# Prompt attention with undivided probabilities: the reciprocals of the sums go through memory, and the results of a pair of heads are multiplied by them

## The chip, the cores and the metric

The kernel runs on one core of one Trainium2 chip. The metric is the device time of one execution in microseconds (us). A core has a matrix engine (PE, with a separate sequence of weight loads, PEld), a vector engine (DVE), an engine for activation functions and copies (ACT), a general one (POOL), and one that mostly issues transfers (SP). A transfer (DMA) is issued by the instruction stream of one of these engines; the rows call the issuing side ACTq, SPq and so on. Memory is DRAM; work happens in the core's own SBUF, and the PE writes into PSUM banks.

## The reference

One step of a layer with two feed-forward halves, a mixer, and norms around each, for a prompt of 1024 positions and a group of samples. Its mixer has a forgetting attention with 8 heads of 64, and a gated linear attention. The part that matters here is the forgetting attention of the prompt:

```python
def fox_prompt(q, k, v, logf):                   # B=1, T=1024, H=8, D=64
    c = jnp.swapaxes(jnp.cumsum(logf, axis=1), 1, 2)
    ...
        s = (jnp.einsum('bqhd,bkhd->bhqk', qb, k) * scale
             + cb[..., :, None] - c[..., None, :])
        mask = (start + jnp.arange(Q_BLOCK))[:, None] >= k_pos[None, :]
        p = jax.nn.softmax(jnp.where(mask, s, -jnp.inf), axis=-1)
        return jnp.einsum('bhqk,bkhd->bqhd', p, v)
```

All of it is float32. The softmax divides each row of exponentials by its sum before the product with `v`.

## The kernel before, in words

**The main stream.** The kernel walks through feed-forward half 1, projection, mixer output and feed-forward half 2. Nearly all of its PE time is matrix products with weights (`mm`, L230). A weight tile of 128x1024 arrives raw from memory (`wr`, 2 buffers), is split by ACT into a rounded part (`wh`, a cast, L213, 3 buffers) and by DVE into the rest (`wl`, L213, 3 buffers); the PE then multiplies with both parts.

**Background pieces.** Prompt attention does not have a stage of its own. It is written as Python generators that `yield` after each small piece. As the main stream advances, it calls `tick(us)` with its own estimate of the time of what it just wrote; that adds to a due count, and for each whole unit of the count one piece of the background is written. `together` takes one piece from each of its generators in turn. Prompt attention for the query chunks 0 and 1 (`fox((0, 1), ...)`, L2083) is written beside the projection, with the linear attention joining later; chunks 2 and 3 (`fox((2, 3), ...)`, L1774) are written beside the second feed-forward half, in turn with the linear attention `gla`. After everything has been written, a scheduler chooses the order of the instructions of each engine; each engine then works strictly in its own order.

**One head of attention.** A chunk has 256 queries, two blocks of 128. For a head h and a chunk c:

- `fox_load` has SP load keys and queries (`ka`, `kb`, `qa`, `qb`), and values (`v`) for every second head.
- `fox_scores`, once per block i: the PE writes the scores `s` (128 queries x n keys, L1429 to L1432; n is 128 to 1024). The DVE takes the maximum (L1434), ACT the exponential into `p` with the sum of each row beside it (L1435), the DVE the reciprocal of that sum (L1436), and ACT multiplies all of `p` by that reciprocal, one per partition (L1437). There are 2 buffers of `p` (`fp`).
- `fox_turn`: the PE transposes up to four 128x128 pieces of `p` into the one PSUM bank `tp` (L1447), and ACT copies them to `pT` (L1449). There are 96 such copies.
- `fox_out`: the PE multiplies `v` with `pT` into `po` (L1463): 64 rows (the head's dimensions) x 256 queries; except in chunk 0, the even and the odd blocks of keys are summed in the two halves of the partitions. ACT copies one half to SBUF (`pl`, L1468), and DVE adds the other (L1469); in chunk 0 ACT copies alone (L1465). An even head goes to partitions 0 to 63 and an odd one to 64 to 127 of one tile, so a pair of heads makes one tile of 128x256.

For chunks 0 and 1 that tile is a part of the next stage's input, `y` (the `put` of L2083's caller). For chunks 2 and 3 it is a tile `mo` with 2 buffers, and after an odd head `done` has SP store it to `mixd` in memory (L1768); `mixd` is loaded as the next stage's input when the attention is over.

There are 4 chunks x 8 heads x 2 blocks = 64 blocks, 32 heads and 16 pairs.

Of the kernel before, what the change touches and what calls it, by code (L numbers as in the profile page):

```python
# [8 lines left out]
F32 = mybir.dt.float32  # L9
# [3 lines left out]
AF = mybir.ActivationFunctionType  # L13
ALU = mybir.AluOpType
# [4 lines left out]
P = 128  # L19
# [41 lines left out]
def together(*gens):  # L61

    live = list(gens)
    while live:
        for g in list(live):
            if next(g, live) is live:
                live.remove(g)
            else:
                yield
# [819 lines left out]
class StepA(Step):  # L889
    def setup_a(self):  # L890
        cp, nc = self.const, self.nc
        dr = self.dram
        self.qs = dr.tile([2, 4, P, T], F32, name="qs")
        self.ks = dr.tile([2, 4, P, T], F32, name="ks")
        self.vs = dr.tile([4, P, KB, P], F32, name="vs")
        self.vss = dr.tile([4, TS, P], F32, name="vss")
        self.augs = dr.tile([8, 2, TP], F32, name="augs")
        self.cns = dr.tile([2, 8, TS], F32, name="cns")
        self.afs = dr.tile([2, 8, NB * NPG, P], F32, name="afs")
        self.gqs = dr.tile([2, P, T], F32, name="gqs")  # L900
        self.gks = dr.tile([2, P, T], F32, name="gks")
        self.gbs = dr.tile([2, P, T], F32, name="gbs")
        self.ggs = dr.tile([4, P, T], F32, name="ggs")
        self.gvs = dr.tile([9, P, 512], F32, name="gvs")
        self.zero = cp.tile([P, 1], F32, name="zero")
        nc.vector.memset(self.zero, 0.0)
        self.gS = cp.tile([P, 2, P], F32, name="gS")
        self.cend = cp.tile([8, 4], F32, name="cend")

# [430 lines left out]
QC = [(0, 256), (256, 256), (512, 256), (768, 256)]  # L1340
# [15 lines left out]
class StepB(StepA):  # L1356
# [57 lines left out]
            nc.sync.dma_start(self.v[:, :nk // P, :], self.vs[h // 2, :, :nk // P, :])  # L1414
        return ka, kb, qa, qb, self.v

    def fox_scores(self, c, i, ld, B, w):

        nc = self.nc
        ka, kb, qa, qb, _ = ld  # L1420
        g = QC[c][0] // P + i
        n = (g + 1) * P
        qs = slice(i * P, i * P + P)
        sp = self.ps.tile([P, w], F32, name=self.uid("s2"), tag="S", bufs=1024 // w)
        p = B.tile([P, w], F32, name=self.uid("p"), tag="p", bufs=self.fp)
        for o in range(0, n, 512):
            m = min(512, n - o)
            end = o + m == n
            nc.tensor.matmul(sp[:, o:o + m], qa[:, qs], ka[:, o:o + m], start=True, stop=False)  # L1429
            nc.tensor.matmul(sp[:, o:o + m], qb[:, qs], kb[:, o:o + m], start=False, stop=not end)  # L1430
            if end:
                nc.tensor.matmul(sp[:, g * P:n], self.identr, self.cmask, start=False, stop=True)  # L1432
        mx = B.tile([P, 4], F32, name=self.uid("fm"), tag="fm", bufs=4)
        nc.vector.tensor_reduce(out=mx[:, 0:1], in_=sp[:, :n], op=ALU.max, axis=AX.X, negate=True)  # L1434
        nc.scalar.activation(out=p[:, :n], in_=sp[:, :n], func=AF.Exp, bias=mx[:, 0:1], accum_out=mx[:, 1:2])  # L1435
        nc.vector.reciprocal(mx[:, 2:3], mx[:, 1:2])  # L1436
        nc.scalar.activation(out=p[:, :n], in_=p[:, :n], func=AF.Copy, scale=mx[:, 2:3])  # L1437
        return p

    def fox_turn(self, c, i, k0, p, pT):  # L1440
# [10 lines left out]
    def fox_out(self, c, h, v, pT, B, put):  # L1451

        nc = self.nc
        q0 = QC[c][0]
        e = h % 2
        r, x = slice(64 * e, 64 * e + 64), slice(64 - 64 * e, 128 - 64 * e)
        po = self.aux("po")
        last = q0 // P + 1
        one = last == 1
        for k in range(last + 1):  # L1460
            s = slice(0, 256) if k < last else slice(P, 256)
            out = po[r if one or k % 2 == 0 else x, s]
            nc.tensor.matmul(out, v[:, k, r], pT[:, k, s], start=(k == 0 or (k == 1 and not one)), stop=(k == last or (k == last - 1 and not one)))  # L1463
        if one:
            nc.scalar.copy(put(r, h // 2, q0), po[r, :256])  # L1465
            return
        t = B.tile([P, 256], F32, name=self.uid("pl"), tag="pl", bufs=1)
        nc.scalar.copy(t[r], po[x, :256])  # L1468
        nc.vector.tensor_tensor(out=put(r, h // 2, q0), in0=po[r, :256], in1=t[r], op=ALU.add)  # L1469

    def fox(self, cs, B, put, w, done=None):

        heads = [(c, h) for c in cs for h in range(8)]
        todo = [(k, i) for k in range(len(heads)) for i in range(2)]
        order = list(todo)
        loads, probs, turned = {}, {}, set()

        def issue():
            if not todo:
                return False  # L1480
            k, i = todo[0]
            j = order.index((k, i))
            if j - self.fp >= 0 and order[j - self.fp] not in turned:
                return False
            del todo[0]
            probs[k, i] = self.fox_scores(*heads[k][:1], i, loads[k], B, w)
            if i == 1 and k + 1 < len(heads):
                loads[k + 1] = self.fox_load(*heads[k + 1], B, w)
            return True

        loads[0] = self.fox_load(*heads[0], B, w)
        yield
        yield
        while issue():
            yield
        for k, (c, h) in enumerate(heads):
            pT = B.tile([P, w // P, 256], F32, name=self.uid("pT"), tag="pT", bufs=2)
            for i in range(2):
                for k0 in range(0, QC[c][0] // P + i + 1, 4):
                    self.fox_turn(c, i, k0, probs[k, i], pT)  # L1500
                    yield
                turned.add((k, i))
                while issue():
                    yield
            self.fox_out(c, h, loads[k][4], pT, B, put)
            if done is not None and h % 2:
                done(h // 2, QC[c][0])
            yield

    def gla_prep(self, ti, B):  # L1510

# [230 lines left out]
    def second(self, p4):  # L1742

        nc = self.nc
        self.ps, closep = self.pool("psX", space=PSUM)
        X, close = self.pool("X", side="right")
        self.rate = RATES
        yield from self.sample(X, self.ps)
        nc.sync.dma_start(self.mixd[:, :4, TP - HALF:], self.mixs)
        close()  # L1750
        p4.close_pages()
        closep()
        self.ps, closep = self.pool("psB1", space=PSUM)
        B, close = self.pool("B1", side="right")
        self.rate = RATE1
        self.naux, self.fp = 2, 2
        self.setup_b(B, TP)
        self.states(B)
        yield
        mo = {}  # L1760

        def put(r, a, q0):
            if r.start == 0:
                mo[a] = B.tile([P, 256], F32, name=self.uid("mo"), tag="mo", bufs=2)
            return mo[a][r]

        def done(a, q0):
            nc.sync.dma_start(self.mixd[:, a, q0 - HALF:q0 - HALF + 256], mo[a])  # L1768

        def gput(ti, t):  # L1770
            o = ti * P - HALF
            nc.sync.dma_start(self.mixd[:, 4:, o:o + t.shape[-1]], t)

        yield from together(self.fox((2, 3), B, put, TP, done), self.gla((4, 5, 8, 6, 7), B, gput))  # L1774
        close()
        closep()
        self.ps, _ = self.pool("ps5", keep=True, space=PSUM)
        self.banks = dict(col=("col", 1), col2=("col", 1), rows=("rows", 1))
        self.ncw, self.ssb, self.xb = NCW, 3, XB
        R, _ = self.pool("R", keep=True, side="right")  # L1780
        self.ub = [R.tile([P, KB, H1N], F32R, name=f"ub2{i}") for i in range(2)]
        p4.y = R.tile([P, KB, H1N], F32, name="y1")
        p4.R = R
        for c0, n in CH[2:]:
            s = slice(c0 - HALF, c0 - HALF + n)
            nc.sync.dma_start(p4.y[:, :, s], self.mixd[:, :, s])
        for _ in range(4):
            yield
        for c0, n in CH[2:]:
            s = slice(c0 - HALF, c0 - HALF + n)  # L1790
            for a in range(0, KB, 2):
                self.split(self.ub[0][:, a:a + 2, s], self.ub[1][:, a:a + 2, s], p4.y[:, a:a + 2, s])
                yield
# [467 lines left out]
```

## Time and profile before

| what | value |
|---|---|
| median of 3 runs | 2278.36 us |
| lowest and highest | 2270.86 and 2279.23 us |
| the profiled execution, its own time | 2268.31 us |
| its span (first to last instruction) | 2266.5 us |
| granted clock of the PE | 0.999 |

The profile is of one execution. Its busy times are per engine; issuing instructions are not counted as busy. A row of the waits view reads "who waited <- for what: us in total, times, longest". A row of the timeline or of the chain reads "start us, length us, what". A row of a line's view reads "engine, instruction, count: shortest/median/longest ns, first to last start". A matmul's end is modelled, so a PE that seems busy may be waiting for short moments; waits of the weight loads (PEld) show more of that.

### The profile page before, as it was taken

The numbers are of one execution on the slowest core, as the hardware profiler recorded it, in microseconds if no ns is written. First come the engines' busy times: TensorE is split into PE (matmuls) and PEld (weight loads), VectorE is DVE, ScalarE is ACT, GpSimd is POOL, SyncE is SP. The second block draws the span as 40 slices with busy tenths as digits, with TensorE's granted clock in tenths as the row PEclk, the third lists the DMA queues.
The fourth block names the chain that finished last, engine by engine and source line by source line (L and its number), as shares of the span: only waits on it lengthen the run. The fifth ranks groups of instructions, "written<-read, shape, count | busy, mean of one in ns | idle before, by whom it ended". The sixth has DMA issues, their size and how long they took to land.

```text
span 2266.5 us, 40596 instructions
## 1 busy us (share of the span) xinstructions
PE 2221.6 (98%) x15056; PEld 1982.9 (87%) x15056; DVE 1538.3 (68%) x2678; ACT 1031.2 (45%) x1787; POOL 625.8 (28%) x570
## 2 busy tenths in 40 slices
PE   9999999999999999999999999999999999999998
PEld 8898888999999877889898677777777989999998
DVE  7878886876777875476455333357775588678866
ACT  6544445433344465655345322236565546333433
POOL 2433332442223322011322312311110135234412
PEclk9999999999999999999999999999999999999999
DMA  5332223322233576564556899855554553224324
GB/s 185 123 103 98 98 99 130 98 82 88 93 113 124 166 256 194 182 191 128 188 181 203 300 346 333 316 159 146 166 151 137 194 174 114 97 89 140 103 83 137
DMA packets 201991, 357.26 MB, mean 158 GB/s; under 512 B 27265, under 2 KB 100546, under 8 KB 201410
## 3 DMA queue, kind: packets, MB, share of 16 engines
q1 hardware_dynamic: 185890, 316.36, 43.1%
q0 software_dynamic: 6544, 21.50, 2.6%
q10 hardware_dynamic: 9360, 16.81, 2.1%
q8 instruction: 120, 1.97, 0.4%
q14 instruction: 77, 0.63, 0.1%
HBM read 308.93 MB, written 45.65 MB: 156 GB/s over the span
## 4 chain that ended last, share of the span: by engine, by line
PE 48%; DVE 7%; issue 5%; ACT 3%; DMA 2%; POOL 1%; ACTq 0%; SPq 0%; DVEq 0%; POOLq 0%
PE mm L230 32%; PE mm L698 3%; DVE wl L213 3%; PE mx L698 2%; PE po L1463 1%; PE sp L1201 1%; PE po L1239 1%; PE tp L1447 1%; ACT wh L213 1%; DMA wr<-in_wd 1%; PE pa L1596 1%; PE s L1429 1%; PE s L1430 1%; PE pS L1639 1%; DMA wr<-in_wout 0%
## 5 line engine op out<-in xcount | busy, mean ns | idle before, releaser
L213 DVE TENSOR_TENSOR wl<-wr,wh 128x1024 fp32r<-128x1024 f32 (+1 forms) x251 | 290.2, 1158 | 181.3 <-ACT wh L213 179.7
L230 PE MATMUL mm<-ua,wh 128*128 128x512 f32 (+2 forms) x1328 | 412.1, 393 | 1.0 <-ACT ua L213 0.6
L213 ACT CAST wh<-wr 128x1024 fp32r<-128x1024 f32 (+1 forms) x251 | 245.2, 979 | 315.0 <-PE mm L230 165.2
L230 PE MATMUL mm<-ub,wh 128*128 128x256 f32 (+3 forms) x1760 | 371.6, 306 | 1.8 <-ACT st L968 0.8
L230 PE MATMUL mm<-hl,wh 128*128 128x256 f32 (+2 forms) x1006 | 330.8, 330 | 0.7 <-DVE hl L213 0.6
L230 PE MATMUL mm<-hh,wh 128*128 128x256 f32 (+2 forms) x958 | 320.7, 336 | 9.6 <-DVE y L646 5.7
L230 PE MATMUL mm<-hh,wl 128*128 128x256 f32 (+2 forms) x958 | 315.6, 330 | 2.2 <-DVE wl L213 2.2
L230 PEld LDWEIGHTS mm<-ub,wh 128*128 128x128 f32 (+1 forms) x1760 | 281.8, 189 | 11.7 <-issue 5.3
L230 PEld LDWEIGHTS mm<-ua,wh 128*128 128x128 f32 (+1 forms) x1328 | 237.3, 188 | 56.8 <-issue 13.1
L230 PE MATMUL mm<-ub,wl 128*128 128x256 f32 (+2 forms) x864 | 258.5, 299 | 1.0 <-DVE wl L213 1.0
L698 PE MATMUL mm<-ub,wh 128*128 128x288 f32 (+1 forms) x1328 | 258.3, 290 | 0.0
L230 PE MATMUL mm<-ua,wl 128*128 128x512 f32 (+1 forms) x656 | 252.1, 385 | 0.0
L698 PEld LDWEIGHTS mm<-ub,wh 128*128 128x128 f32 x1328 | 210.9, 189 | 0.0
L646 DVE TENSOR_TENSOR y<-y,mm 128x256 f32<-128x256 f32 (+2 forms) x275 | 137.0, 524 | 108.4 <-PE mm L230 108.1
L230 PEld LDWEIGHTS mm<-hh,wh 128*128 128x128 f32 x958 | 181.0, 189 | 31.1 <-issue 7.4
L230 PEld LDWEIGHTS mm<-hl,wh 128*128 128x128 f32 x1006 | 190.5, 190 | 15.0 <-DVE hl L213 1.8
L230 PEld LDWEIGHTS mm<-hh,wl 128*128 128x128 f32 x958 | 181.5, 189 | 16.8 <-DVE wl L213 3.7
L698 PE MATMUL mm<-ub,wl 128*128 128x288 f32 (+1 forms) x664 | 192.8, 290 | 0.0
L698 PE MATMUL mm<-ua,wh 128*128 128x288 f32 (+1 forms) x912 | 177.9, 290 | 0.8 <-ACT wh L213 0.8
L230 PEld LDWEIGHTS mm<-ub,wl 128*128 128x128 f32 x864 | 163.1, 189 | 2.8 <-DVE wl L213 1.4
L230 PEld LDWEIGHTS mm<-ua,wl 128*128 128x128 f32 x656 | 123.4, 188 | 26.6 <-issue 2.4
L698 PEld LDWEIGHTS mm<-ua,wh 128*128 128x128 f32 x912 | 144.6, 189 | 1.3 <-ACT wh L213 1.0
(336 smaller groups left out, 4189.1 us busy)
## 6 DMA issues: line engine op xcount, KB each, us to landing
wr<-in_wgu SPq DMA_DIRECT2D x72, 512.0 KB
wr<-in_wd SPq DMA_DIRECT2D x68, 512.0 KB
pr<-in_ck SPq DMA_DIRECT2D x112, 256.0 KB
wz<-in_wgu SPq DMA_DIRECT2D x100, 256.0 KB
wr<-in_win SPq DMA_DIRECT2D x50, 512.0 KB
pr<-in_cv ACTq DMA_DIRECT2D x64, 256.0 KB
wx<-in_wgu SPq DMA_DIRECT2D x50, 256.0 KB
wr<-in_wout SPq DMA_DIRECT2D x24, 512.0 KB
```

Of the source, the lines that this page charges most:

```text
L213: for ins in (self.nc.scalar.copy(hi, src), self.nc.vector.tensor_tensor(out=lo, in0=src, in1=hi.bitcast(F32), op=ALU.subtract)):
L230: ins = self.nc.tensor.matmul(*a, **kw)
L646: self.note(nc.vector.tensor_tensor(out=yk, in0=yk, in1=pds[d2, c0, e], op=ALU.add))
L698: nc.tensor.matmul(ps, a, x, start=(k == 0 and j == 0), stop=(k == KB // 2 - 1 and j == len(ops) - 1))
L1201: nc.tensor.matmul(sp[32 * a:32 * a + 32, 256 * hf:256 * hf + 256], qz[p % 2][:, a, s, :], raw[:, :, a * P:(a + 1) * P], start=False, stop ...
L1239: nc.tensor.matmul(po[r], pT[:, t, r], raw[:, :, a * P:(a + 1) * P], start=(t == 0), stop=False)
L1429: nc.tensor.matmul(sp[:, o:o + m], qa[:, qs], ka[:, o:o + m], start=True, stop=False)
L1430: nc.tensor.matmul(sp[:, o:o + m], qb[:, qs], kb[:, o:o + m], start=False, stop=not end)
L1447: nc.tensor.transpose(tp[:, k * P:(k + 1) * P], p[:, (k0 + k) * P:(k0 + k + 1) * P], self.ident)
L1463: nc.tensor.matmul(out, v[:, k, r], pT[:, k, s], start=(k == 0 or (k == 1 and not one)), stop=(k == last or (k == last - 1 and not one)))
L1596: nc.tensor.matmul(pa[:n, l - l0, :, a, :n // 2], E[:, l, a, :n], self.qd[:, l, a, :, :n // 2], start=True, stop=True)
L1639: nc.tensor.matmul(pS[:, a, :], km[:n, a, :], v[:n, a * 256:(a + 1) * 256], start=True, stop=True)
```

## The change

The exponentials are no longer divided. Instead:

- After the reciprocal, ACT issues a transfer of the 128 reciprocals of the block (one float32 per partition) to `rec`, a new tensor of 4 x 8 x 256 floats in memory, where the 256 of a head lie in a row.
- Ahead of `fox_out`, ACT issues a transfer that reads the head's row of `rec` into 64 partitions of a tile of 128x256, each partition getting the same row. An even head fills the lower half, an odd head the upper. The tile takes the name `pl` and the one buffer that the copy of `fox_out` had.
- `fox_out` now copies the one half straight to the place of the result, and adds the other half there.
- `whole` multiplies the tile of a pair by the tile of reciprocals: one DVE instruction of 128x256 per pair. In chunks 2 and 3 it then calls `done`. It is written one head later than the pair is finished (after the first turn of the next head's second block), and for the last pair after two more empty pieces.

```diff
@@ __init__
+        self.rec = dr.tile([4, 8, 256], F32, name="rec")
@@ fox_scores
-    def fox_scores(self, c, i, ld, B, w):
+    def fox_scores(self, c, h, i, ld, B, w):
...
         nc.scalar.activation(out=p[:, :n], in_=sp[:, :n], func=AF.Exp, bias=mx[:, 0:1], accum_out=mx[:, 1:2])
         nc.vector.reciprocal(mx[:, 2:3], mx[:, 1:2])
-        nc.scalar.activation(out=p[:, :n], in_=p[:, :n], func=AF.Copy, scale=mx[:, 2:3])
+        nc.scalar.dma_start(self.rec[c, h, i * P:i * P + P].rearrange("(p o) -> p o", o=1), mx[:, 2:3])
         return p
@@ fox_out
-        t = B.tile([P, 256], F32, name=self.uid("pl"), tag="pl", bufs=1)
-        nc.scalar.copy(t[r], po[x, :256])
-        nc.vector.tensor_tensor(out=put(r, h // 2, q0), in0=po[r, :256], in1=t[r], op=ALU.add)
+        t = put(r, h // 2, q0)
+        nc.scalar.copy(t, po[x, :256])
+        nc.vector.tensor_tensor(out=t, in0=po[r, :256], in1=t, op=ALU.add)
@@ fox
-            probs[k, i] = self.fox_scores(*heads[k][:1], i, loads[k], B, w)
+            probs[k, i] = self.fox_scores(*heads[k], i, loads[k], B, w)
...
+        rows, late = {}, []
+
+        def whole(c, h):
+            a, q0 = h // 2, QC[c][0]
+            t = put(slice(0, P), a, q0)
+            self.nc.vector.tensor_tensor(out=t, in0=t, in1=rows["t"], op=ALU.mult)
+            if done is not None:
+                done(a, q0)
+
         for k, (c, h) in enumerate(heads):
             pT = B.tile([P, w // P, 256], F32, name=self.uid("pT"), tag="pT", bufs=2)
             for i in range(2):
                 for k0 in range(0, QC[c][0] // P + i + 1, 4):
                     self.fox_turn(c, i, k0, probs[k, i], pT)
                     yield
+                    if i == 1 and k0 == 0 and late:
+                        whole(*late.pop())
                 turned.add((k, i))
                 while issue():
                     yield
+            if h % 2 == 0:
+                rows["t"] = B.tile([P, 256], F32, name=self.uid("pl"), tag="pl", bufs=1)
+            self.nc.scalar.dma_start(rows["t"][64 * (h % 2):64 * (h % 2) + 64, :], self.rec[c, h:h + 1, :].to_broadcast([64, 256]))
             self.fox_out(c, h, loads[k][4], pT, B, put)
-            if done is not None and h % 2:
-                done(h // 2, QC[c][0])
+            if h % 2:
+                late.append((c, h))
             yield
+        yield
+        yield
+        whole(*late.pop())
@@ put (chunks 2 and 3)
-            if r.start == 0:
+            if r.start == 0 and r.stop < P:
                 mo[a] = B.tile([P, 256], F32, name=self.uid("mo"), tag="mo", bufs=2)
```

The order of the instructions on each engine, as built, shows the change at three places. Lines of the changed kernel are one higher than before up to the loop of `fox` (the exponential is L1436 there, the copy to `pT` L1450) and 17 or 18 higher behind it. L1438 is the write of the reciprocals, L1519 the read of a row, L1502 the product. The numbers behind names are those of buffers and differ between the two builds.

First, ACT in the second stage, for the last blocks of a head of chunk 3. `po` holds the attention's result, `wh` is a weight cast. Before:

```order
L213 CAST wh_19570<-wr_19279 128x1024
L1435 ACTIVATE p_19395,fm_19401<-s_2939_19394,fm_19401 128x1024
L213 CAST hh_18236<-sg_19134 128x512
L1468 COPY pl_19433<-po_19424 64x256
L1437 ACTIVATE p_19395<-p_19395,fm_19401 128x1024
L1449 COPY pT_19455<-tp_19456 128x4x128
L1449 COPY pT_19455<-tp_19465 128x3x128
L1449 COPY pT_19455<-tp_19514 128x4x128
L1435 ACTIVATE p_19478,fm_19484<-s_2959_19477,fm_19484 128x896
L1449 COPY pT_19455<-tp_19524 128x4x128
L1437 ACTIVATE p_19478<-p_19478,fm_19484 128x896
```

In the changed kernel:

```order
L213 CAST wh_19606<-wr_19312 128x1024
L1436 ACTIVATE p_19430,fm_19436<-s_2934_19429,fm_19436 128x1024
L213 CAST hh_18264<-sg_19168 128x512
L1469 COPY mo_19470<-po_19461 64x256
L1438 DMA rec<-fm_19436 128x1
L1450 COPY pT_19491<-tp_19492 128x4x128
L1519 DMA pl_19459<-rec 64x256
L1450 COPY pT_19491<-tp_19501 128x3x128
L1450 COPY pT_19491<-tp_19550 128x4x128
L1436 ACTIVATE p_19514,fm_19520<-s_2954_19513,fm_19520 128x896
L1450 COPY pT_19491<-tp_19560 128x4x128
L1438 DMA rec<-fm_19520 128x1
```

The write stands where the scaling stood, directly ahead of a copy to `pT`, and the read stands two rows behind the write, with one copy to `pT` between them and another behind it.

Second, ACT in the first stage, for a head of chunk 0. Before:

```order
L1435 ACTIVATE p_9524,fm_9528<-s_1460_9523,fm_9528 128x256
L1437 ACTIVATE p_9524<-p_9524,fm_9528 128x256
L1465 COPY y_9335<-po_9559 64x256
L1449 COPY pT_9572<-tp_9573 128x128
L213 CAST wh_9671<-wr_9548 128x1024
```

In the changed kernel:

```order
L1436 ACTIVATE p_9525,fm_9529<-s_1460_9524,fm_9529 128x256
L1438 DMA rec<-fm_9529 128x1
L1466 COPY y_9336<-po_9562 64x256
L1519 DMA pl_9560<-rec 64x256
L1450 COPY pT_9575<-tp_9576 128x128
L213 CAST wh_9675<-wr_9549 128x1024
```

A read now stands ahead of the copy to `pT`, and the cast of the next weights behind both.

Third, the DVE in the second stage. `at`, with its predicated copies, belongs to the linear attention. Before:

```order
L1434 TENSOR_REDUCE fm_19544<-s_2964_19537 128x1
L1576 TENSOR_TENSOR at_19558<-ident,pd_19561 128x512
L213 TENSOR_TENSOR wl_19735<-wr_19441,wh_19734 128x1024
L1436 RECIPROCAL fm_19544<-fm_19544 128x1
L1469 TENSOR_TENSOR mo_19435<-po_19582,pl_19591 64x256
L1599 COPY_PREDICATED at_19558<-lmask_17625,pa_19599 128x4x64
L1599 COPY_PREDICATED at_19558<-lmask_17625,pa_19599 128x8x32
```

In the changed kernel:

```order
L1435 TENSOR_REDUCE fm_19580<-s_2959_19573 128x1
L1594 TENSOR_TENSOR at_19594<-ident,pd_19597 128x512
L1437 RECIPROCAL fm_19580<-fm_19580 128x1
L1470 TENSOR_TENSOR mo_19470<-po_19619,mo_19470 64x256
L1617 COPY_PREDICATED at_19594<-lmask_17650,pa_19634 128x4x64
L1502 TENSOR_TENSOR mo_19470<-mo_19470,pl_19459 128x256
L1617 COPY_PREDICATED at_19594<-lmask_17650,pa_19634 128x8x32
```

The product of the pair stands two rows behind the addition of the pair's second head, in spite of being written one head later, and the subtraction for `wl` stands further ahead in this piece.

## The prediction

> Line numbers are those of the kernel before unless "changed" stands with them. I take about 0.5% (11.4 us of the 2278.36 us median) as what a measurement of this kernel can tell from no change.
>
> **What bounds the kernel now.** I read the page's busy times first, then the two stretches in which prompt attention runs, then what the PE waited for in them.
>
> ```profile
> span 2266.5 us, 40596 instructions
> PE 2221.6 (98%) x15056; PEld 1982.9 (87%) x15056; DVE 1538.3 (68%) x2678; ACT 1031.2 (45%) x1787; POOL 625.8 (28%) x570
> ```
>
> The PE is idle for 2266.5 - 2221.6 = 44.9 us in all. Every instruction that the change touches lies between 860 and 1735 us, in two stages; by the windows view (length, then busy us and count of PE, PEld, DVE, ACT, POOL) these are:
>
> ```profile
> 860.00:1090.00 230.00, 226.16 (x1490) 199.78 (x1489) 136.71 (x358) 137.62 (x292) 22.51 (x39) 1.00 0.55 171
> 1505.00:1735.00 230.00, 223.11 (x1317) 171.76 (x1316) 162.19 (x386) 134.48 (x232) 25.99 (x39) 1.00 0.53 153
> ```
>
> PE idle there is 3.8 and 6.9 us, 10.7 in all, and the matmuls do not change. So the time moves only by what is taken from, or added to, the PE's waits. The waits view gives those that end with ACT, three PE rows and three of the weight loads in the second stage, which show more because a matmul's modelled end covers short gaps:
>
> ```profile
> PE tp L1447 <- ACT pT L1449: 3.2, 4, 0.9
> PE tp L1447 <- ACT p L1437: 1.7, 2, 1.4
> PE s L1429 <- ACT p L1435: 0.9, 2, 0.6
> PEld tp L1447 <- ACT pT L1449: 10.7, 22, 1.4
> PEld s L1429 <- ACT p L1435: 2.8, 6, 1.0
> PEld tp L1447 <- ACT p L1437: 2.3, 2, 1.8
> ```
>
> The transposes wait far oftener for ACT's copy out of the single transpose bank (`pT`, L1449) than for the scaled probabilities (`p`, L1437). One such wait, ACT and PE side by side:
>
> ```profile
> 1661.39 1.01 ACT L1435 ACTIVATE p<-s,fm 128x896 f32<-128x896 f32 x1 [3.00 <-DVE fm L1434]
> 1662.39 0.58 ACT L1449 COPY pT<-tp 128x512 f32<-128x512 f32 x1
> 1663.02 0.66 PE L1447 MATMUL tp<-ident,p 128*128 128x128 f32 x4 [0.93 <-ACT pT L1449]
> ```
>
> The copy stood behind an Exp in ACT's order, and the Exp behind the DVE's maximum. What stands directly ahead of a `pT` copy on ACT is therefore what decides; how busy ACT is on average does not.
>
> **What is removed.** The 64 scalings:
>
> ```profile
> L1437 ACT ACTIVATE p<-p,fm x64: 396/768/1152, 870.7 to 1721.9; 128x128 f32<-128x128 f32 x8, 128x256 f32<-128x256 f32 x8, 128x384 f32<-128x384 f32 x8, 128x512 f32<-128x512 f32 x8
>   DVE fm L1436: 13.2, 24
> ```
>
> 64 x 0.768 = 49 us of ACT, and 13.2 us in which ACT stood for the reciprocal. The PE pays 1.7 us directly for them (2 waits above). They also delay copies: in the built order before, 27 of the 96 `pT` copies stand directly behind a scaling, 27 x 0.77 = 20.8 us.
>
> **What is added on ACT's queue.** Per block one write of 128 x 4 bytes, per head one read of a row into 64 partitions. Prices of an issue: ACT's own in the stage between, and a 64-row load of SP.
>
> ```profile
> L1093 ACTq DMA_DIRECT2D pr<-in_cv x64: 339/340/1682, 1284.4 to 1469.2; - x64
> L1407 SPq DMA_DIRECT2D qa<-qs x64: 444/455/1119, 862.7 to 1698.0; - x64
> ```
>
> 64 x 0.34 + 32 x 0.455 = 36.3 us, against the 49 removed. The write waits for the same reciprocal as the scaling did, so the 13.2 us stay. The new wait is the read's: it can be issued only when the write of its own head's second block has landed, and ACT takes nothing after it until then. Landing, from the start of an issue, stands in the chain of waits:
>
> ```profile
> 936.38 2.39 DMA ka<-ks
> 948.74 2.24 DMA ks<-st
> 1564.60 2.09 DMA gb<-gbs
> ```
>
> I take 2.24, the store. A write of 128 single words is not in the trace; nearest are these, both with far longer rows, so for it I allow 2.09 to twice 2.24. In the built order after, 78 ACT rows stand between write and read over the 32 heads, 2.4 per head, 0 to 5. At ACT's mean row of (137.62 + 134.48) / (292 + 232) = 0.52 us they take 1.25 us, and 2.1 us of elapsed time since ACT is busy 59% of these stages. With the write's own 0.34 the read is reached some 1.6 to 2.4 us after the write began. That leaves a stand w of 0 to 0.6 us per head; I take 0.3. For the eight heads with at most one row between, about 1.4. A gain is not possible here.
>
> In the order after, 25 `pT` copies stand directly behind a write and 17 behind a read (changed L1438, L1519). Time directly ahead of `pT` copies: 25 x 0.34 + 17 x (0.455 + 0.3) = 21.3 us, against 20.8 before. Net +0.5 us, of which the PE sees between 27% (26 weight-load and PE waits on 96 copies) and all: 0.1 to 0.5. Behind the read also wait the casts of the weights (`wh`, 3 directly), which the three split buffers cover: ACT itself waited for the PE before `wh` in the second stage:
>
> ```profile
> ACT wh L213 <- PE mm L230: 12.0, 6, 4.6
> ```
>
> Without that cover a `wh` cast would pass on w itself, 3 x 0.3 = 0.9 us.
>
> [...]
>
> **What is added on the DVE.** 16 products of 128x256, all operands in SBUF; the nearest row is such a product, and the row beside it is the addition that stays:
>
> ```profile
> 1082.44 0.43 DVE L1572 TENSOR_TENSOR kn<-gk,gq 128x256 f32<-128x256 f32 x1
> 1082.89 0.43 DVE L1469 TENSOR_TENSOR y<-po,pl 64x256 f32<-64x256 f32 x1
> ```
>
> 16 x 0.43 = 6.9 us, in stages where the DVE has 460 - 298.9 = 161 us free: 0. A product waits for its row's read; it is placed at least 50 instructions of the program (4 us or more at some 10 per us) behind that read's issue, longer than the 2.39 us of a load, so I price its stand at 0; without cover, 2.39 us once per pair would keep the subtractions for `wl` waiting behind it. The copy that went to a tile of its own now goes where the sum goes: same sizes, 0.
>
> **What is moved on SP's queue.** The store of a pair's result comes one head later. SP waited for that result before as well:
>
> ```profile
> SPq L1768 <- DVE mo L1469: 16.4, 7, 6.7
> ```
>
> The built order puts the store again behind the product; its two buffers hold a pair longer, and a pair lasts some 25 us. The next loads of keys and weights behind it have 2 raw weight tiles as cover: 0, or up to 2 us if one comes late. At the end of the second attention stage two more steps and one product follow; the PE then runs on for 27 us on its own work, so 2 us more there cost 0:
>
> ```profile
> 1727.43 27.12 PE mm L230 x117
> 1728.76 2.12 SPq L1786 DMA_DIRECT2D y<-mixd  x2
> ```
>
> **The sum**, against the profiled execution (2268.31 us, span 2266.5): -1.7 (waits for the scaling) +0.3 (ahead of copies) +0 (DVE, SP) = -1.4, so 2266.9. That execution was below all three timed runs (2270.86 to 2279.23); carried to their median, 2278.36 - 1.4 = 2277.0. Unknown costs alone give -4.4 to +7: the low end takes the weight loads' waits for `p` (2.3, with 0.4 of the first stage) beside the 1.7; the high end is -1.7 + 5.6 (w = 0.6 passed on whole, 17 x 0.6 - 4.6) + 3.2 (four of the eight short heads at 1.4 instead of 0.6).
>
> **Rivals.**
> 1. *ACT stands at the read until the write lands (slower).* For it: the read stands close behind the write, and `pT` copies behind the read. Against: ACT idles 41% of the stages. Passed on whole, the PE gets 25 x 0.34 + 17 x (0.455 + w) - 20.8 = 17w - 4.6. It decides (over 11.4) from w = 0.94 us. At w = 1.6, a landing of some 3.6 us: +22.6 whole, about +16 at 70%: 2294 us. At the landing of twice 2.24 that I allow, w is about 2.5, and 70% of 37.9 is +27: 2305 us, the far end of this rival.
> 2. *ACT runs ahead and the PE's waits on it go (faster).* If all of PEld's waits on ACT in the second stage go (10.7 + 2.8 + 2.3 = 15.8) and some 2 us of the first: -17, 2261 us. For it: 49 us of ACT gone and each block's chain from Exp to transposes shorter by about 0.9 us. Against: the shown wait had an Exp and a DVE maximum ahead, which stay, and issues take back 36.3 of the 49.
> 3. *The change is real but the order is reshuffled around it.* Some 190 of 12,798 PE rows stand elsewhere, all in these stages; the PE's idle time there (10.7) is the size of what that could move: ±6 us, inside "no change".
>
> **How the numbers follow.** Forecast (no change, with the third rival) 0.62; first rival 0.20; second 0.18. The time is 2277 us. The range must reach into both rivals: 2260 to 2294, of which the forecast's own part is 2268 (2278.36 - 4.4 - 6 of the third rival) to 2286 (+7). Faster by over 0.5% 0.18, within 0.62, slower 0.20.
>
> **What would show it.** Right: PE idle in the two stages stays within about 7 to 16 us; ACT's busy time falls by about 49 us; the reads' stands show as short idle times before `pT` copies released by a DMA or an issue. The first rival shows as PE or PEld waits on `pT` well above 14 us with DMA or issue ahead of ACT's copies. The second shows as that row near zero. Wrong altogether: a wait outside the two stages, or SP loading weights late because it stands for a small transfer of ACT's.

## The result, and the profile after

The changed kernel takes 2526.57 us (median of 4 runs, 2523.5 to 2537.01) against 2278.8 us: a ratio of 1.111, 95% interval 1.109 to 1.113. That is 248 us slower, where 2277 us was forecast. The profiled execution is one of 2523.5 us with a span of 2521.7 us, 255.2 us longer than the span before.

The page of the changed kernel, first its span and busy times, then the row of the granted PE clock in 40 slices:

```profile
span 2521.7 us, 40806 instructions
PE 2290.6 (91%) x15056; PEld 2034.4 (81%) x15056; DVE 1543.9 (61%) x2694; ACT 986.3 (39%) x1723; POOL 623.6 (25%) x570
...
PEclk9999999999999987878999999998898999999999
```

The PE does the same 15056 matmuls. It is idle for 231.1 us instead of 44.9 (+186.2), and it is busy for 69.0 us more; the two make the 255.2. The additional busy time goes with the clock, which falls in the slices of the two attention stages (0.83 and 0.88 in the windows below, 1.00 before).

Stage by stage, in the windows view (length, then busy us and count of PE, PEld, DVE, ACT, POOL, the granted clock, the share of the 16 DMA engines, GB/s). The windows shown before were 230 us each; these hold 6% and 8% more matmuls:

```profile
860.00:1255.00 395.00, 275.72 (x1579) 239.99 (x1577) 146.33 (x375) 125.25 (x272) 23.92 (x40) 0.83 0.64 106
1660.00:2010.00 350.00, 275.86 (x1418) 212.05 (x1417) 181.39 (x418) 117.28 (x216) 24.48 (x39) 0.88 0.65 116
```

Nearly all of the loss lies there: matched matmul by matmul, the changed kernel is 0.6 us late at the start of the first stage, 153 us late behind it, 158 us at the start of the second, 254 us behind it.

What the waits say, of engines first and then of SP's queue:

```profile
PEld tp L1448 <- ACT pT L1450: 135.4, 30, 12.1
PE tp L1448 <- ACT pT L1450: 125.9, 23, 11.7
ACT pT L1450 <- DMA rec<-fm: 54.5, 10, 7.8
SPq L1409 <- DMA rec<-fm: 33.0, 7, 6.9
```

The transposes waited 3.2 us (PE) for ACT's copies before, in 4 waits in the second stage; now 125.9 us in 23, and the copies in turn wait for the write of the reciprocals. The view of the two new lines gives issue times (shortest/median/longest ns), and the longest wait of the read in ACT's queue:

```profile
L1438 ACTq DMA_DIRECT2D rec<-fm x64: 321/326/702, 871.7 to 1969.4; - x64
L1519 ACTq EVENT_SEMAPHORE  x45: 17/38/9089, 889.5 to 1973.3; - x45
```

Issuing is as cheap as assumed (0.33 us). Landing is not. The chain of waits in the second stage has, with start and length:

```profile
1847.35 8.96 DMA rec<-fm
1891.41 8.31 DMA rec<-fm
1910.76 10.97 DMA rec<-fm
1954.04 13.21 DMA rec<-fm
```

Over the 64 writes, the time from the start of an issue to the last completion is 6.67 us at least, 8.93 in the median, 15.78 at most. One of them in the timeline (start, length, engine; in brackets the idle time before and its releaser):

```profile
1910.76 0.33 ACTq L1438 DMA_DIRECT2D rec<-fm  x1
...
1912.46 0.58 ACT L1450 COPY pT<-tp 128x512 f32<-128x512 f32 x1 [1.54 <-DVE at L1617]
...
1913.85 0.49 PE L1448 MATMUL tp<-ident,p 128*128 128x128 f32 x3
...
1921.96 0.46 ACTq L1519 DMA_DIRECT2D pl<-rec  x1
1922.47 0.48 ACT L1450 COPY pT<-tp 128x384 f32<-128x384 f32 x1 [9.42 <-DMA mixd<-mo]
...
1923.00 1.12 PE L1448 MATMUL tp<-ident,p 128*128 128x128 f32 x4 [5.01 <-ACT pT L1450]
```

The write is issued at 1910.76, ACT does one copy, and then takes nothing until the read can go at 1921.96; ahead of the copy behind it ACT was idle for 9.42 us, and the PE then stood for 5.01 us. (The releaser named for the copy is a store that ended nearby; the read ahead of it waits for `rec`.) The packets of this write, 144 of 4 bytes, are all shown between 1914.75 and 1916.36, but the 16 updates of its semaphore that tell of its completion come between 1916.12 and 1921.73: half of the landing time comes after the last packet. Over the 32 heads, the time between the end of ACT's work ahead of a read and the issue of the read is 228.5 us, 7.14 us per head.

The second finding is that other transfers suffer too. The loads of 64 rows of 1 KB by SP (`qa`) landed in 3.17 us in the median before and in 8.16 now. The view of the DMA queues, for the first stage of the kernel before (first fence) and of the changed one (second), shows packets, MB and the time of the packets of SP's queue as a share of 16 engines over the window (230 and 395 us):

```profile
q1 hardware_dynamic: 31427, 39.01, 54.5%
```

```profile
q1 hardware_dynamic: 32749, 40.68, 60.5%
```

For about the same bytes that is 0.545 x 230 x 16 = 2006 engine-us before and 0.605 x 395 x 16 = 3824 after. It is not that every packet takes longer: over the whole span 60 packets of SP's queue took more than 1 us before, 71 us together, and 1343 after, 3149 us together; the 4-byte packets of ACT's queue take 9 ns in the median.

### The profile page after: what moved, and what is told of

It is laid out like the page before. It is cut to its first block, busy times and chain, and to the rows that moved or that the text cites. A ratio compares the mean times of both kernels' runs of the same rounds, so it can differ in the third digit from the quotient of the medians.

```text
span 2521.7 us, 40806 instructions
## 1 busy us (share of the span) xinstructions
PE 2290.6 (91%) x15056; PEld 2034.4 (81%) x15056; DVE 1543.9 (61%) x2694; ACT 986.3 (39%) x1723; POOL 623.6 (25%) x570
## 5 line engine op out<-in xcount | busy, mean ns | idle before, releaser
L230 PE MATMUL mm<-ua,wh 128*128 128x512 f32 (+2 forms) x1328 | 426.7, 404 | 2.2 <-issue 1.3
L230 PE MATMUL mm<-ub,wh 128*128 128x256 f32 (+3 forms) x1760 | 384.5, 313 | 2.6 <-ACT st L969 1.0
L230 PEld LDWEIGHTS mm<-ub,wh 128*128 128x128 f32 (+1 forms) x1760 | 292.8, 196 | 13.7 <-issue 6.3
L230 PEld LDWEIGHTS mm<-ua,wh 128*128 128x128 f32 (+1 forms) x1328 | 245.7, 195 | 61.0 <-issue 16.4
L230 PE MATMUL mm<-ua,wl 128*128 128x512 f32 (+1 forms) x656 | 258.9, 395 | 0.0
L1448 PE MATMUL tp<-ident,p 128*128 128x128 f32 x288 | 59.5, 324 | 125.9 <-ACT pT L1450 125.9
L230 PEld LDWEIGHTS mm<-ub,wl 128*128 128x128 f32 x864 | 168.4, 195 | 2.7 <-DVE wl L213 1.4
L1448 PEld LDWEIGHTS tp<-ident,p 128*128 128x128 f32 x288 | 40.9, 165 | 142.6 <-ACT pT L1450 135.4
```

The costliest lines, as they stand in the source:

```text
L230: ins = self.nc.tensor.matmul(*a, **kw)
L1448: nc.tensor.transpose(tp[:, k * P:(k + 1) * P], p[:, (k0 + k) * P:(k0 + k + 1) * P], self.ident)
```

## The experiments

Two theories at first. **A**: the write lands late, ACT stands at the read, and the copies to `pT` and the casts behind it come late (the first rival of the prediction). **B**: the single-word writes hold up the other transfers, so that keys and weights come late whether ACT stands or not. Differences below are to the kernel before in the same set of runs. Where a run's results are not normalised, its expectation says what is left out.

### Writes without reads

```diff
-            self.nc.scalar.dma_start(rows["t"][64 * (h % 2):64 * (h % 2) + 64, :], self.rec[c, h:h + 1, :].to_broadcast([64, 256]))
...
-            self.nc.vector.tensor_tensor(out=t, in0=t, in1=rows["t"], op=ALU.mult)
+            self.nc.vector.tensor_tensor(out=t, in0=t, in1=self.ones[:, :1].to_broadcast([P, 256]), op=ALU.mult)
...
```

> The changed kernel without its reads: the 64 writes of 128 single words stay, the products of a pair multiply by a constant one, so the results are not normalised. No instruction of ACT waits for a write any more. Theory A (ACT stands at the read until the write has landed, and copies to pT and weight casts wait behind it): nearly all of the +248 us goes, 2265 to 2300 us, and the PE is idle 4 to 15 us in each of the two stages. Theory B (the single-word writes hold up the other transfers of the same engines, so that keys and weights come late): most of it stays, over 2400 us, and SP's transfers in the stages still take about twice the engine time for the same bytes (3824 against 2006 engine-us in the first stage).

Measured: 2426.1 us against 2269.1, ratio 1.069 (1.065 to 1.072). So 157 us stay with no read for ACT to stand at: theory B carries the larger part. The queue view of the first stage, here 355 us long, has

```profile
q1 hardware_dynamic: 32864, 41.08, 73.0%
```

which is 0.73 x 355 x 16 = 4146 engine-us for SP's transfers, against 2006 before. In the chain of this run stand loads of SP whose like landed in 3.17 us (`qa`) and 3.28 us (`kb`) in the median before:

```profile
905.57 8.87 DMA qa<-qs
...
1686.77 12.02 DMA kb<-ks
```

Beside the slower landing, the waits of SP's queue in this run show a second way in which the writes hold up the loads:

```profile
SPq L1409 <- DMA rec<-fm: 40.0, 9, 8.9
SPq L1412 <- DMA rec<-fm: 14.9, 3, 7.0
SPq L1408 <- DMA rec<-fm: 12.0, 4, 6.7
```

These lines load keys and queries and need nothing of `rec`. The traces show the landing of a transfer as up to 16 updates of one semaphore. In the traces of the kernel before, of the changed one and of this run, the transfers of SP and ACT share eight such semaphores, mostly in turn (by time of issue, 1199 of 1260 transfers before and 1108 of 1356 in the changed kernel took the next one), and by the landings recorded none was issued before the one ahead of it on its semaphore had landed (at the least 0.016 us lie between the two). So here a write that landed late also kept back the transfer that came next on its semaphore, and what stood behind that on its issuer (40.0 us in 9 waits at L1409 above). Over all its lines SP stood 101.9 us for `rec` in this run, 129.6 in the changed kernel and not at all before. The expectation that no instruction of ACT waits for a write any more was wrong: ACT's issues stood in this rotation too, 68 us in all and 9.1 of them for writes of `rec`, against 5 us before. No run here separates these stands from the slower transfers; the 157 us are both.

### Reads without writes

```diff
+        nc.sync.dma_start(self.rec.rearrange("c h q -> (c h q)").rearrange("(p k) -> p k", p=P), self.ones[:, :64])
...
-        nc.scalar.dma_start(self.rec[c, h, i * P:i * P + P].rearrange("(p o) -> p o", o=1), mx[:, 2:3])
```

> The changed kernel without its 64 writes: the row tensor is filled once at the start with ones, so the results are not normalised; the 32 reads and 16 products stay. Both theories: 2260 to 2290 us, since neither a stand at a write nor single-word writes are left. If the reads themselves (64 rows from one kilobyte of memory) or their issue on ACT cost something, it shows here: above 2300 us.

Measured: 2267.66 us against 2269.1, ratio 0.999 (0.998 to 1.000). The removed scaling, the 32 reads and their issues on ACT, the 16 products, the later stores and the new order come to -1.4 us together, which can't be told from nothing. That each of them by itself is near nothing is not shown; a gain and a cost could cancel. What is left of the 248 us belongs to the 64 writes and the waits for them.

### The length of the pieces

```diff
-        self.rec = dr.tile([4, 8, 256], F32, name="rec")
+        self.rec = dr.tile([4, 8, 256, P], F32, name="rec")
...
-        nc.scalar.dma_start(self.rec[c, h, i * P:i * P + P].rearrange("(p o) -> p o", o=1), mx[:, 2:3])
+        nc.scalar.dma_start(self.rec[c, h, i * P:i * P + P, :], p[:, :P])
...
```

> The changed kernel with one size changed: the write carries 512 bytes per partition (the first 128 exponentials of the row) instead of 4, still 128 rows and as many transfers, and the read takes one kilobyte that both writes of a head touch, so it waits for both as before; the results are not normalised. If the length of the piece is the cause (theories A and B both through the slow single words): the write lands in 2 to 3.5 us instead of 9, and the time is 2265 to 2330 us. If a write to memory followed by a read lands late whatever its pieces (theory C): still over 2400 us. Under A with a landing of 2.5 us, a stand of 0.5 us per head, some +5 to +20 us are left.

Measured: 2274.54 us against 2269.1, ratio 1.0025 (1.0014 to 1.0036). With 128 times the bytes in as many pieces, the write lands in 2.26 us in the median, one of them in the chain of waits of this run being

```profile
1577.15 2.40 DMA rec<-p
```

so theory C (a write that is read back is slow whatever its pieces) falls. ACT stands 20.6 us at the reads in all, 0.64 us each.

### The read one head later

```diff
+        def fetch(c, h):
+            if h % 2 == 0:
+                rows["t"] = B.tile([P, 256], F32, name=self.uid("pl"), tag="pl", bufs=1)
+            r = slice(64 * (h % 2), 64 * (h % 2) + 64)
+            self.tc.keep_in_program_order(self.nc.scalar.dma_start(rows["t"][r, :], self.rec[c, h:h + 1, :].to_broadcast([64, 256])))
...
-                    if i == 1 and k0 == 0 and late:
-                        whole(*late.pop())
+                    if i == 1 and k0 == 0 and k:
+                        fetch(*heads[k - 1])
...
```

> The changed kernel, all computed, but each read is kept in the order in which it is written, one head later (6 to 10 instructions of ACT behind the write instead of 0 to 5, some 6 us or more), and the pair's product another half head later. Theory A: most of the stands go, 2270 to 2340 us. Theory B: the single-word writes still hold up keys and weights, over 2400 us. In between, the two shares can be read: what is left here beside the run without reads is the stand.

Measured: 2472.29 us against 2269.1, ratio 1.089 (1.086 to 1.092). The stand at the reads is nearly gone (15.0 us over the 32, from 228.5), but only 45 of the 248 us go with it (203 stay). By this run the stand is worth 45 us, by the one without reads 91 (248 - 157); here the reads themselves land late (7.74 us in the median), and the products and stores with them, so that neither figure is the stand alone. In both the larger part stays as long as the single-word writes stay.

### The place of the words

The length and the place of the pieces had changed together. This run keeps single words and changes their place alone.

```diff
-        self.rec = dr.tile([4, 8, 256], F32, name="rec")
+        self.rec = dr.tile([4, 8, 256, 128], F32, name="rec")
...
-        nc.scalar.dma_start(self.rec[c, h, i * P:i * P + P].rearrange("(p o) -> p o", o=1), mx[:, 2:3])
+        nc.scalar.dma_start(self.rec[c, h, i * P:i * P + P, :1], mx[:, 2:3])
...
```

> The changed kernel with one thing moved: each of the 128 single words of a write goes to a row of memory of its own, 512 bytes apart, instead of all into the same 512 bytes; the read takes one kilobyte that both writes of a head touch (its other words are filled once with ones by a few transfers of POOL, so the results are not normalised). Theory D (a single-word piece written to memory is slow by itself): the write still lands in about 9 us and the time is 2450 to 2560 us. Theory E (the 128 words get in each other's way because they share one short stretch of memory): the write lands in 2 to 4 us and the time is 2268 to 2310 us.

Measured: 2282.74 us against 2270.11, ratio 1.0057 (1.0037 to 1.0077). The same 8192 words from the same partitions, by the same instructions, land in 2.90 us in the median, and SP's transfers are undisturbed:

```profile
q1 hardware_dynamic: 31264, 38.90, 53.1%
```

(over 240 us, 2039 engine-us). So it is neither the number of pieces nor their length by itself: 128 single words side by side are what is slow. Of the 248 us, 235 go with their place. SP's packets of more than 1 us are down to 123, 143 us together.

### Pieces of 64 bytes

```diff
+        self.rec = dr.tile([4, 8, 256, 16], F32, name="rec")
...
+        nc.scalar.dma_start(self.rec[c, h, i * P:i * P + P, :], p[:, :16])
...
```

> The changed kernel with 64 bytes per partition in the write (the first 16 exponentials), the rows side by side, still 128 pieces; the read waits for both writes of a head as before; the results are not normalised. Theory D in the form that every piece under 512 bytes is slow: above 2400 us. Theory E, or D for single words alone: within 10 us of the run with 512-byte pieces (2274.5 us), since no two pieces share 64 bytes. In between: the cost falls with the length of the piece.

Measured: 2272.93 us against 2270.11, ratio 1.0014 (1.0004 to 1.0024), landing 2.33 us in the median. Pieces of 64 bytes side by side land like those of 512 (2.26 us).

### Words nearer to each other

The edit is that of words 512 bytes apart, with another length of the rows of `rec`:

```diff
-        self.rec = dr.tile([4, 8, 256, 128], F32, name="rec")
+        self.rec = dr.tile([4, 8, 256, 16], F32, name="rec")    # 64 bytes apart; 4 for 16 bytes apart
```

> As the run with words 512 bytes apart (2282.7 us, landing 2.9 us), with the words 64 bytes apart, so that 8 of them share a stretch of 512 bytes. If words conflict only within 64 bytes or less: 2275 to 2290 us and a landing of 2.5 to 3.5 us. If they conflict within 512 bytes: 8 words share one, so less than the 128 of the changed kernel but seen: 2295 us or more, landing over 3.5 us.

> The same with the words 16 bytes apart: 32 of them share 512 bytes, 4 share 64. If the conflict is within 64 bytes: a landing of 3 to 4.5 us and 2285 to 2330 us. If within 512 bytes: a landing of 4 to 6 us and 2320 to 2420 us. If the words are served one after the other whatever the stretch is, it would have shown at 512 bytes apart.

Measured: 64 bytes apart 2286.27 us against 2273.6, ratio 1.0054 (1.0035 to 1.0072), landing 2.56 us; 16 bytes apart 2294.71 us, ratio 1.0091 (1.0072 to 1.0109), landing 3.17 us. Both fall where a conflict within 64 bytes was expected to put them. So the conflict isn't one of words that share 512 bytes, of which 32 do at 16 bytes apart. Most of it appears between 16 bytes apart and side by side. Which unit of the memory or of the transfer it belongs to is not settled by these runs.

### Fewer words

```diff
-        nc.scalar.dma_start(self.rec[c, h, i * P:i * P + P].rearrange("(p o) -> p o", o=1), mx[:, 2:3])
+        nc.scalar.dma_start(self.rec[c, h, i * P:i * P + 32].rearrange("(p o) -> p o", o=1), mx[:32, 2:3])
```

(on top of the run without reads)

> The run of the writes alone (2426 us) with a write of 32 of the 128 reciprocals, side by side in 128 bytes; no reads, so the results are not normalised. If words of one stretch are served one after the other, the landing falls in proportion, from 9.5 us to about 1.5 + (9.5 - 1.5) / 4 = 3.5 us, and the time to 2275 to 2310 us. If one shared stretch costs the same however many words go to it: still above 2380 us.

Measured: 2325.38 us against 2273.6, ratio 1.0225 (1.0207 to 1.0244), landing 5.21 us instead of 9.51. A quarter of the words costs a third of the time (52 of 157 us). The cost grows with the words, but the landing fell less than in proportion (3.5 us expected, of which 1.5 us for what does not depend on the words was the author's estimate; no run shows it; the shortest fully recorded landing of any transfer is 1.63 us in the trace before and 1.61 in that of the changed kernel), so that words served strictly one after the other do not explain all of it.

### A repair: rows made on the DVE

```diff
-        nc.vector.reciprocal(mx[:, 2:3], mx[:, 1:2])
-        nc.scalar.dma_start(self.rec[c, h, i * P:i * P + P].rearrange("(p o) -> p o", o=1), mx[:, 2:3])
-        return p
+        return p, mx
...
+                    if k0 == 0:
+                        a, b = (pT[:, QC[c][0] // P + 1, o:o + 32] for o in (64 * i, 64 * i + 32))
+                        self.nc.vector.reciprocal(a, probs[k, i][1][:, 1:2].to_broadcast([P, 32]))
+                        self.nc.vector.transpose(b, a)
+                        self.nc.scalar.dma_start(self.rec[c, h, i * P:i * P + P].rearrange("(b q) -> b q", q=32), b[0:P:32, :])
```

> The changed kernel, all computed, with the reciprocals turned into rows by the DVE before the write (32x32 blocks, in columns of pT that the block does not use), so that a write has 4 pieces of 128 bytes instead of 128 single words; the write is issued at the first turn of its block. 256 pieces in all instead of 8192. Theories D and E: 2266 to 2280 us against 2269 before; with the run without writes at 2267.7 nothing lower than about 2265 is to be had. If 128-byte pieces are as slow as single words, the landing stays above 5 us and ACT stands at the read: 2300 to 2400 us.

Measured: 2273.94 us (median of 10: 2270.75 to 2277.9, and one of 5161.61 that nothing here explains) against 2270.11, ratio 1.0014 (1.0004 to 1.0024), landing 2.08 us. It computes everything, and 4 pieces of 128 bytes in place of 128 words take away nearly all of the loss.

### Later reads without slow writes

Two runs join edits shown above: the later read with the 512-byte pieces, and the later read with the turned rows.

```diff
+            self.tc.keep_in_program_order(self.nc.scalar.dma_start(rows["t"][r, :], ...))
...
+        nc.scalar.dma_start(self.rec[c, h, i * P:i * P + P, :], p[:, :P])                                                      # first
+                        self.nc.scalar.dma_start(self.rec[c, h, i * P:i * P + P].rearrange("(b q) -> b q", q=32), b[0:P:32, :])  # second
```

> 512-byte pieces in the write and the read kept one head later, so that neither slow pieces nor a stand at the read are left; the results are not normalised. If the 5.4 us by which the run with 512-byte pieces is above before are ACT's stand at the read (landing 2.26 us, close behind the write): 2265 to 2271 us. If they are the transfers' own load: 2272 to 2278 us.

> All computed: the reciprocals turned into rows by the DVE (4 pieces of 128 bytes in a write) and the read one head later. No conflict and no stand left: 2265 to 2271 us, ratio to before 0.998 to 1.001, as in the run without writes (0.999) and the one with 512-byte pieces and later reads (0.9992). Lower than 0.997 would mean that the removed scaling is worth more than those runs show.

Measured: 2267.98 us against 2270.11, ratio 0.9992 (0.9982 to 1.0001), for the first; no read stands any more, and the 5.4 us that the 512-byte pieces cost have gone with ACT's stand. For the second 2278.88 us against 2273.6, ratio 1.0017 (1.0008 to 1.0026): not better than the turned rows with the early read, and not what was expected. Why isn't known; its writes land in 2.24 us, no read stands, and in its profile 6.5 of the 14.5 us by which it is behind at the end arise between the two stages, where the change has no instruction. No version found here beats the kernel before by more than can be measured.

## Why the prediction was wrong

**What bounds the kernel** was right: with the writes out of the way, the rest of the change moves the time by 0.1%. The run without writes gave -1.4 us (interval about -5 to 0). That this is also the sum's -1.4 is luck: the sum was for a kernel with writes that land in 2.24 us. The run that comes nearest to that, 512-byte pieces that land in 2.26 us, gave +5.4 (3 to 8), since reads stood 0.64 us per head where 0.3 was taken. With 0.64 the prediction's own terms, passed on whole, give -1.7 + 17 x 0.64 - 4.6 = +4.6. ACT's busy time fell by 44.9 us (49 foreseen), DVE's rose by 5.6 (6.9 foreseen), the issues cost 0.33 and 0.46 us as priced, and products, stores and the later order cost nothing that shows in the run without writes.

**The step that failed** is the landing of the write: "I take 2.24, the store", with up to twice that allowed. The trace of the change has 8.93 us, 6.67 at the least. The step took the two nearest rows by what they are called, a store and a load of long rows, and put a factor of two on them, though nothing in the trace had the form of this transfer: 128 single words from 128 partitions, side by side in memory. The factor had no row behind it. With the measured 7.14 us per head in place of w = 0.3, the prediction's own formula, 17w - 4.6, gives 117 us for full pass; the runs put the stand at 45 to 91, between the 27% (32 us) and all that the prediction allowed. That mechanism was the first rival, with a chance of 0.20 and a price of 16 to 27 us, and where the writes land early its formula was good: in the six runs with an early read and a landing of 2.1 to 3.2 us, w was 0.5 to 1.4 us, and -1.7 + 17w - 4.6 is within 5 us of what was measured in each (+2.5 against +3.8 for the turned rows, +17.1 against +21.1 for words 16 bytes apart).

**What was missing altogether** is the larger part. The prediction priced the writes by what stands behind them on ACT and never asked what they do to the other transfers that the DMA engines carry. That is +157 us where no read waits for a write. The term for SP's queue, "0, or up to 2 us if one comes late", failed with it: loads that landed in 3.17 us took 8.16, while SP stood for `rec` as well (33.0 us in 7 waits at one line of its loads, 129.6 over all lines).

**A second missing term** is the clock. Behind its stands the PE went on at half the granted clock: all 32 stands of more than 1.5 us in the two stages of the changed kernel (1.71 to 11.69 us) have a stretch at 0.50 within 3.41 us of their end. The windows view of the changed kernel around the stand shown above:

```profile
1914.00:1923.00 9.00, 3.99 (x27) 3.45 (x25) 3.00 (x5) 0.53 (x2) 0.00 (x0) 0.95 1.01 142
1923.00:1926.00 3.00, 3.00 (x11) 2.71 (x12) 0.16 (x1) 1.53 (x3) 0.00 (x0) 0.50 0.62 234
1926.00:1930.00 4.00, 4.00 (x18) 3.42 (x17) 0.31 (x1) 1.08 (x2) 0.00 (x0) 0.62 0.21 15
1930.00:1936.00 6.00, 6.00 (x40) 4.45 (x39) 4.79 (x9) 2.84 (x4) 1.57 (x1) 1.00 0.47 100
```

The PE is busy for 3.99 of 9 us, then runs at 0.50, and is back at 1.00 after 1930. So a stand cost its own length and part of the next microseconds: the PE was busy for 140.8 us at half the clock, half of which accounts for the 69 of the 255 us by which it is busier. The 31 half-rate stretches of the two stages last 3.4, 6.8, 10.2 or 13.7 us. In the 3.41 us ahead of each of them the PE was busy for 0 to 1.67 us, and one came behind a stand of 1.71 us.

**The length of the pieces** did not decide by itself: 64-byte pieces landed in 2.33 us, 512-byte pieces in 2.26, 4 pieces of 128 bytes in 2.08 and single words 512 bytes apart in 2.90, against 8.93 for single words side by side (medians).

**The other rivals.** ACT's head start (the second) brings nothing that can be measured: the run without writes is its best case, at 0.999. The order of that run (the third) costs nothing that can be measured either. The list of what would show the rivals was right: `pT` waits far above 14 us with a DMA ahead, and, under "wrong altogether", SP's loads late because it stands for a small transfer of ACT's.

## What to carry to other kernels

A transfer whose form isn't in the trace can't be bounded by twice the nearest row (here 8.93 us against 2.24); give it its own measurement, or a price for the case that it is slow for everyone on the same engines. A column of single words written side by side to memory is such a form: turn it into a few rows before it leaves the core (2.08 us), or put the words apart (2.56 to 3.17 us at 16 to 512 bytes), and read it back well behind the write (one head later the stands at the reads fell from 228.5 to 15.0 us). And a scaling that the profile shows off the critical path is not worth removing, however long it keeps its engine busy: taking 49 us off ACT was worth 1.4 us here (0 to 5), net of the reads and products that came in its place.

## What was unexpected about the hardware

- 128 single words written side by side land in 8.93 us (median of 64); 16 bytes apart in 3.17, 64 apart in 2.56, 512 apart in 2.90; 64-byte pieces side by side in 2.33; 4 pieces of 128 bytes in 2.08.
- While such writes are under way, other transfers of the core take far longer (64 rows of 1 KB: 3.17 us in the median before, 8.48 beside the writes alone), although the packets of the writes are shown as short ones (9 ns in the median) and other packets as the long ones (of SP's queue 1493 over 1 us, against 60 before). Spacing the words by 512 bytes brings 3.14.
- Stands of the PE of 1.7 to 11.7 us were followed by 3.4 to 13.7 us at half the granted clock (32 stands and 31 such stretches in the two stages).
